# Grouped query pairs share value products, attention's scratch changes place, and norm squares are added on VectorE, in a two-layer hybrid trunk

## The chip, the core and the metric

The kernel runs on one core of a Trainium2 chip. The metric is the device time of one execution in microseconds (us), the median of several runs. The engines are TensorE (PE: matrix products; its weight loads are listed as PEld), VectorE (DVE), ScalarE (ACT), GpSimd (POOL) and SyncE (SP), whose queue starts all transfers. PSUM is the memory that TensorE writes, in banks; SBUF is the working memory.

## The reference

Two layers over 256 context tokens and 512 latent tokens of width 1024. In each layer a modulated RMS norm feeds one wide projection. Its columns go to four mixers (a bidirectional state-space layer "S5", a gated short convolution, neighbourhood attention, windowed grouped-query attention), to their gates and to merge gates. Each mixer's output is gated, projected and added into a sum that is gated by channel; one output projection and a gated residual end the layer. The parts that matter here, cut:

```python
def _rmsnorm(x, g):
    y = xf * lax.rsqrt(jnp.mean(xf * xf, axis=-1, keepdims=True) + EPS)
...
# grouped-query attention: 8 query heads, 2 key/value heads, blocks of 128 queries,
# keys: the block and its neighbours in a window of 128, the context, and a sink logit
pr = jax.nn.softmax(jnp.concatenate([s_lat, s_ctx, sink_l], axis=-1), axis=-1)
o = (jnp.einsum("bkgqs,bskd->bqkgd", pr[..., :span], v_i)
     + jnp.einsum("bkgqc,bckd->bqkgd", pr[..., span:span + n_ctx], v_ctx))
...
gated = y * jax.nn.silu(z[name + "_gate"])
contrib = jax.nn.sigmoid(z["merge_" + name]) * (gated @ p["w_br"][k])
```

The last layer computes its context tokens only as far as keys, values and states need them.

## The kernel before

Activations lie transposed: 128 channels on the partitions, tokens along the free dimension, the 1024 channels in 8 tiles. Large products run at a reduced-precision type in three terms: activations and weights are split into a high and a low part (`split`, line 228, a ScalarE cast and a VectorE subtraction), and `dense` (line 190) issues high x high, high x low and low x high. A unit of projection is 24 products over 512 latent tokens (bank `pl`) and, where the context is wanted, 24 over its 256 tokens (`pc`). Weights come through two buffers `wraw`.

A layer has two stages. `front` (line 685) runs attention. For each of 8 attention units (4 of neighbourhood attention, 4 grouped ones, each a pair of query heads) `weave` (line 777) interleaves query tiles of attention with projection units of the coming attention unit, convolution and gates. `back` (line 1350) runs the branch products (`merge`, line 1314), the S5 layer and the output projection, with the next layer's state-space factors (`s5_ahead`) between.

No engine order is written out: the program is traced with priorities, and a planner, which times instructions by a model of its own, fixes each engine's order when the program is built. Attention has a raised priority (`tile_prio`). Each engine then runs its own list in order, and waits on semaphores.

`attend_` (line 563) handles one head and 128 queries: scores into the bank pair `S`, bias and maximum on VectorE (line 576), exponentials on ScalarE (586), normalization on VectorE (588), transposes in blocks of 128 keys into `T` (597), a split into `ph` and `pl_` (two buffers each), and then the value products of line 606: per key block, 64 columns of high values with `ph` and with `pl_`, and 64 columns of low values with `ph`, added up in `o[:64, :128]` of the bank `M`, of which there is one. `store_y` (line 611) copies the sum to `y` on ScalarE (line 624). `M` also takes the sums of squares of the query/key norm (`qk_unit`, line 485) and of the token norm. Query stacks `qs0`, `qs1` have one buffer each and are filled by transfers from `qhi` and `qlo` (line 524).

`norm_stats` (line 351) makes the token norm's scale: ScalarE squares of each of the 8 tiles (line 359), then for each 128 tokens a product of the squares with a column of ones into `M` (line 364), a VectorE reduction over the 8 sums (375), a scalar step (377), the power -1/2 on GpSimd (379), transposes to spread it (382) and a copy (384). Another branch (`rows`) serves the latent tokens at the very start only. `norm_apply` (line 387) then multiplies, modulates and splits, tile by tile. Between the layers the latent tokens are normalized while the output projection still runs over the context for tiles 4 to 7.

SBUF pools are stacked. When the front's pool `at_` closes, the back's pools take its addresses: first `ac_` (accumulators `acc`), then `bm_` (the gated values `gh` and `gl`, loaded from memory). With `reuse_waits="tile"` a new tile waits for the last use of the old tiles that it overlaps. Within a pool, tiles lie in the order in which their names are first asked for.

Of the kernel before, what the change touches and what calls it, by code (L numbers as in the profile page):

```python
# [11 lines left out]
F32 = mybir.dt.float32  # L12
F32R = mybir.dt.float32r
AF = mybir.ActivationFunctionType
OP = mybir.AluOpType
# [3 lines left out]
D = 1024  # L19
SEQ = 512  # L20
CTX = 256
TOK = CTX + SEQ
NEG = -1e30
EPS = 1e-6
# [98 lines left out]
class Net:  # L123
# [227 lines left out]
    def norm_stats(self, pool, xs, q, rows=False):  # L351

        nc = self.nc
# [3 lines left out]
        for k in range(KD):  # L357
# [5 lines left out]
            for b in range(nb):  # L363
                nc.tensor.matmul(sums[:, b * 8 + k:b * 8 + k + 1], sq[:, b * 128:(b + 1) * 128], self.ones[:, 0:1],  # L364
                                 start=True, stop=True)
        t = pool.tile([128, 8], F32, name="ntiny", bufs=4)
        if rows:
# [5 lines left out]
            nc.vector.tensor_copy(t[:, :nb], sums[:, :nb])  # L373
        else:
# [185 lines left out]

    tile_prio = 1500

    def attend_(self, pool, qs, kh, kl, v, qtok, k0, vbs, bias, sink, dst):
# [25 lines left out]
        ph = pool.tile([128, 640], F32R, name="ph", bufs=2)  # L589
        pl = pool.tile([128, 640], F32R, name="pl_", bufs=2)  # L590
        vbs = (*vbs, 0, 1)
        nb = len(vbs)
        for b0 in range(0, nb, 4):
# [5 lines left out]
            self.split(ph[:, c], pl[:, c], T[:, :(b1 - b0) * 128])  # L599
        o = self.ps.tile([128, 512], F32, name="M")  # L600
        i = 0
        for b in range(nb):
            vb = vbs[b]
            c = slice(b * 128, (b + 1) * 128)
            for w, p in ((slice(0, 64), ph), (slice(0, 64), pl), (slice(64, 128), ph)):
                last = nc.tensor.matmul(o[:64, :128], v[:, vb, w], p[:, c], start=i == 0, stop=i == 3 * nb - 1)  # L606
                i += 1
        self.last_pv = last.ins
        dst(o[:64, :128])

    def store_y(self, y, h, j, na):
# [3 lines left out]
        def f(o):  # L615
            a = CTX - self.base
            if j < 0:
# [24 lines left out]
    def na_tiles(self, l, pool, m, parts, A):  # L642
        nc = self.nc
        A["y"] = y = self.tp(pool, "y", bufs=2)
        for h in range(2):
            args = (pool, A["qs"][h], A["kh"][h], A["kl"][h], A["v"][:, :, h])
            for j in range(4):
# [824 lines left out]
```

## Time and profile before

| | |
|---|---|
| median of 3 runs | 2159.69 us |
| the runs | 2159.69, 2160.14, 2150.65 us |
| profiled execution, its own time | 2153.59 us |
| its span in the profile | 2151.7 us |
| mean granted clock of TensorE | 0.982 |
| TensorE busy | 2086.2 us (97%) |
| VectorE busy | 1351.8 us (63%) |
| ScalarE busy | 898.2 us (42%) |
| GpSimd busy | 321.5 us (15%) |

Times inside the span count from its start. The front of layer 0 runs to about 650 us, its back to about 1290, the front of layer 1 to about 1770. A record of a product has the length of its way through the array, so records overlap; the time that a product holds TensorE is the distance to the next start. A product of the full-precision type has two records.

### The profile page before, as it was taken

What the parts mean: (1) busy time and instruction counts of PE and PEld (TensorE: products, weight loads), DVE (VectorE), ACT (ScalarE), POOL (GpSimd) and SP (SyncE); (2) the same over time, 40 slices, a digit from 0 to 9 for tenths busy, and PEclk for the clock granted to TensorE, in tenths of its full rate; (3) what the DMA queues carried; (4) which work ended last, traced back from release to release, by engine and by line L of the source; (5) the groups of instructions that cost most, each with busy time, mean ns of one, the idle gap of its engine ahead of it and who ended that gap; (6) DMA issues with size and microseconds to landing.
All of it is one profiled execution on the core that took longest, in us unless ns stands there. A gap on an engine that the chain in (4) does not pass through costs nothing.

```text
span 2151.7 us, 34689 instructions
## 1 busy us (share of the span) xinstructions
PE 2086.2 (97%) x12868; PEld 1784.2 (83%) x12868; DVE 1351.8 (63%) x2770; ACT 898.2 (42%) x1936; POOL 321.5 (15%) x326
## 2 busy tenths in 40 slices
PE   8899999999999999999899998999999999999999
PEld 3788888898898888888788887888888887878887
DVE  6476767579665778777547764455556655566543
ACT  4454444354643333333333335455445453323331
POOL 1721222232310000000000004222223300000000
PEclk9899999999999999999999989999999999999999
DMA  6353553532424556464254755444333328863542
GB/s 257 118 154 115 155 159 108 155 121 65 136 82 159 148 157 187 131 182 128 83 192 143 241 178 193 132 122 128 95 113 97 118 91 258 263 204 112 167 138 98
DMA packets 165774, 316.45 MB, mean 147 GB/s; under 512 B 59363, under 2 KB 83171, under 8 KB 164837
## 3 DMA queue, kind: packets, MB, share of 16 engines
q1 hardware_dynamic: 165604, 314.24, 47.6%
q8 instruction: 101, 1.65, 0.3%
q14 instruction: 69, 0.56, 0.1%
HBM read 214.09 MB, written 51.31 MB: 123 GB/s over the span
## 4 chain that ended last, share of the span: by engine, by line
PE 69%; DVE 5%; DMA 4%; ACT 2%; issue 1%; SPq 1%; POOL 0%; DVEq 0%; ACTq 0%; POOLq 0%
PE pl L209 36%; PE pc L209 10%; PE S L209 9%; PE M L606 3%; PE T L597 2%; DMA s<-s 2%; PE T L1076 2%; PE S L570 1%; PE T L1150 1%; PE S L572 1%; PE T L1067 1%; PE M L485 1%; PE T L1193 0%; PE T L1192 0%; PE M L364 0%
## 5 line engine op out<-in xcount | busy, mean ns | idle before, releaser
L209 PE MATMUL pl<-hh,whi 128*128 128x512 f32 x1312 | 522.9, 400 | 5.0 <-ACT hh L229 2.2
L209 PE MATMUL pl<-hh,wlo 128*128 128x512 f32 x1312 | 522.0, 398 | 5.5 <-DVE wlo L178 5.5
L209 PE MATMUL pl<-hl,whi 128*128 128x512 f32 x1312 | 522.8, 398 | 1.1 <-DVE hl L230 1.1
L177 ACT CAST whi<-wraw 128x512 fp32r<-128x512 f32 x440 | 271.8, 620 | 505.6 <-PE pl L209 196.6
L178 DVE TENSOR_TENSOR wlo<-wraw,whi 128x512 fp32r<-128x512 f32 x348 | 241.4, 696 | 185.6 <-ACT whi L177 180.3
L209 PEld LDWEIGHTS pl<-hh,wlo 128*128 128x128 f32 x1312 | 247.6, 189 | 58.4 <-DVE wlo L178 6.8
L209 PEld LDWEIGHTS pl<-hh,whi 128*128 128x128 f32 x1312 | 247.8, 189 | 54.6 <-ACT hh L229 3.6
L209 PEld LDWEIGHTS pl<-hl,whi 128*128 128x128 f32 x1312 | 247.9, 189 | 51.1 <-DVE hl L230 2.5
L209 PE MATMUL pc<-hh,whi 128*128 128x256 f32 x768 | 224.3, 292 | 8.5 <-ACT hh L229 4.5
L209 PE MATMUL pc<-hl,whi 128*128 128x256 f32 x768 | 221.2, 288 | 1.0 <-DVE hl L230 0.9
L209 PE MATMUL pc<-hh,wlo 128*128 128x256 f32 x768 | 220.8, 287 | 0.0
L178 POOL TENSOR_TENSOR wlo<-wraw,whi 128x512 fp32r<-128x512 f32 x92 | 127.6, 1390 | 305.2 <-ACT whi L177 259.8
L209 PEld LDWEIGHTS pc<-hh,whi 128*128 128x128 f32 x768 | 147.8, 192 | 17.5 <-ACT hh L229 5.9
L586 ACT ACTIVATE s<-s,stiny 128x512 f32<-128x512 f32 (+2 forms) x160 | 112.5, 703 | 108.9 <-DVE stiny L585 54.6
L209 PEld LDWEIGHTS pc<-hl,whi 128*128 128x128 f32 x768 | 147.6, 192 | 7.3 <-DVE hl L230 2.1
L606 PE MATMUL M<-ph,v 128*64 128x128 f32 x1216 | 147.2, 228 | 4.1 <-ACT y L624 1.8
L209 PEld LDWEIGHTS pc<-hh,wlo 128*128 128x128 f32 x768 | 147.5, 192 | 0.9 <-issue 0.4
L209 PE MATMUL S<-gh,whi 128*128 128x512 f32 (+1 forms) x384 | 138.8, 361 | 2.2 <-DMA gh<-gd 0.8
L209 PE MATMUL S<-gl,whi 128*128 128x512 f32 (+1 forms) x384 | 137.7, 359 | 1.4 <-DMA gl<-gd 1.4
L209 PE MATMUL S<-gh,wlo 128*128 128x512 f32 (+1 forms) x384 | 137.2, 357 | 0.0
L606 PEld LDWEIGHTS M<-ph,v 128*64 128x64 f32 x1216 | 127.2, 138 | 12.0 <-ACT y L624 3.3
L229 ACT CAST ph<-T 128x512 fp32r<-128x512 f32 (+2 forms) x192 | 92.7, 497 | 57.3 <-PE T L597 50.3
(778 smaller groups left out, 3733.6 us busy)
## 6 DMA issues: line engine op xcount, KB each, us to landing
wraw<-wu SPq DMA_DIRECT2D x220, 512.0 KB
wada<-wada SPq DMA_DIRECT2D x40, 512.0 KB
s<-s SPq DMA_DIRECT2D x80, 192.0 KB
bias<-bias SPq DMA_DIRECT2D x64, 128.0 KB
kh<-qhi SPq DMA_DIRECT2D x40, 192.0 KB
kl<-qlo SPq DMA_DIRECT2D x40, 192.0 KB
gh<-gd SPq DMA_DIRECT2D x16, 384.0 KB
gl<-gd SPq DMA_DIRECT2D x16, 384.0 KB
```

Source lines behind the costliest of these rows:

```text
L177: nc.scalar.copy(hi, raw[:, c])
L178: e.tensor_tensor(lo, raw[:, c], hi.bitcast(F32), op=OP.subtract)
L209: mm = nc.tensor.matmul(out[q], a[:, c], b[k][:, s], start=k + n == 0, stop=k == nk - 1 and n == 2)
L229: self.nc.scalar.copy(hi, src)
L485: nc.tensor.matmul(sums[:, 2 * b:2 * b + 2], sq[:, c:c + 128], self.blk1, start=True, stop=True)
L570: nc.tensor.matmul(S[:, 512 - n:512], qa, k[:, CTX + k0 * 64:CTX + k0 * 64 + n], start=i == 0, stop=i == 1)
L572: nc.tensor.matmul(S[:, 512:768], qa, k[:, :CTX], start=i == 0, stop=i == 1)
L586: nc.scalar.activation(s[:, a:e], s[:, a:e], AF.Exp, bias=tn[:, 1:2], accum_out=tn[:, 2:3])
L597: nc.tensor.transpose(T[:, (b - b0) * 128:(b - b0 + 1) * 128], s[:, a + b * 128:a + (b + 1) * 128], self.ident)
L606: last = nc.tensor.matmul(o[:64, :128], v[:, vb, w], p[:, c], start=i == 0, stop=i == 3 * nb - 1)
L1067: nc.tensor.transpose(o[:, g * 128:(g + 1) * 128], win[d][:, g].rearrange("p s i -> p (s i)"), self.ident)
L1076: nc.tensor.matmul(o[:16, g * 128:(g + 1) * 128], X[:, 0, d, g], WO[:, d, g, d:d + 8].rearrange("p k i -> p (k i)"), start=True, stop=True)
```

## The change

Four edits. In the grouped attention units the two heads of a pair, which share keys and values, are now visited in turn for each query tile; their probabilities lie in two halves of one pair of tiles, and one set of products of 128 value columns (high and low) by 256 (both heads' queries) serves both. The rows for low values times low probabilities come along. The upper 64 rows of the result are added to the lower on VectorE as the result is stored. Neighbourhood attention keeps its products and alternates the halves. In `norm_stats` the 8 tiles of squares are added on VectorE and one product per 128 tokens sums over the channels. In `front`, the scratch of convolution and of query normalization is asked for first, so it lies lowest in the pool. The accumulators' pool is opened after `bm_` rather than before.

```diff
@@ norm_stats
-            for b in range(nb):
-                nc.tensor.matmul(sums[:, b * 8 + k:b * 8 + k + 1], sq[:, b * 128:(b + 1) * 128], self.ones[:, 0:1],
-                                 start=True, stop=True)
+            if k == 0:
+                tot = sq
+            elif k == 1:
+                t1 = pool.tile([128, 512], F32, name="nsum", bufs=1)[:, :n]
+                nc.vector.tensor_tensor(t1, tot, sq, op=OP.add)
+                tot = t1
+            else:
+                nc.vector.tensor_tensor(tot, tot, sq, op=OP.add)
...
         else:
-            nc.vector.tensor_reduce(t[:, :nb], sums[:, :8 * nb].rearrange("p (b k) -> p b k", k=8),
-                                    axis=mybir.AxisListType.X, op=OP.add)
-        nc.vector.tensor_scalar(t[:, :nb], t[:, :nb], 1.0 / D, EPS, op0=OP.mult, op1=OP.add)
+            for b in range(nb):
+                nc.tensor.matmul(sums[:, b:b + 1], tot[:, b * 128:(b + 1) * 128], self.ones[:, 0:1], start=True, stop=True)
+            nc.vector.tensor_scalar(t[:, :nb], sums[:, :nb], 1.0 / D, EPS, op0=OP.mult, op1=OP.add)
@@ attend_, and the new values_
-        ph = pool.tile([128, 640], F32R, name="ph", bufs=2)
-        pl = pool.tile([128, 640], F32R, name="pl_", bufs=2)
+        ph, pl = (t[:, half] for t in self.pt)
...
+    def values_(self, v, vbs, half, dsts):
+        nc = self.nc
+        ph, pl = self.pt
+        vbs = (*vbs, 0, 1)
         o = self.ps.tile([128, 512], F32, name="M")
-            for w, p in ((slice(0, 64), ph), (slice(0, 64), pl), (slice(64, 128), ph)):
-                last = nc.tensor.matmul(o[:64, :128], v[:, vb, w], p[:, c], start=i == 0, stop=i == 3 * nb - 1)
-                i += 1
+        for b, vb in enumerate(vbs):
             c = slice(b * 128, (b + 1) * 128)
+            if half is None:
+                for i, p in enumerate((ph, pl)):
+                    last = nc.tensor.matmul(o[:, :256], v[:, vb], p[:, :, c], start=b + i == 0, stop=b == len(vbs) - 1 and i == 1)
+                continue
+            for i, (w, p) in enumerate(((slice(0, 64), ph), (slice(0, 64), pl), (slice(64, 128), ph))):
+                last = nc.tensor.matmul(o[:64, :128], v[:, vb, w], p[:, half, c], start=b + i == 0, stop=b == len(vbs) - 1 and i == 2)
         self.last_pv = last.ins
-        dst(o[:64, :128])
+        for h, dst in enumerate(dsts):
+            dst(o[:, h * 128:(h + 1) * 128], half is None)
@@ store_y
             nc.scalar.copy(d, o)
+            if two:
+                nc.vector.tensor_tensor(d, d, o2, op=OP.add)
@@ na_setup
+        self.pt = [pool.tile([128, 2, 640], F32R, name=n) for n in ("ph", "pl_")]
@@ gqa_tiles
+        for j in (0, 1, 2, 3) + ((-2, -1) if "c" in parts else ()):
...
+            for h in range(2):
...
+                self.attend(pool, A["qs"][h], A["kh"][kv], A["kl"][kv], h, qtok, 2 * k0, vbs, mask, sink)
+                if h == 1:
+                    self.values(v, vbs, None, [self.store_y(y, i, j, False) for i in range(2)])
                 yield
@@ front
+        self.t3(pool, "cvv", bufs=1), self.tp(pool, "cvy", bufs=1)
+        for _ in range(3):
+            self.t3(pool, "qt", bufs=3)
+        for n in ("qhi", "qlo"):
+            self.t3(pool, n, bufs=1, dt=F32R)
         self.attention_constants(pool)
@@ back
             pm = stack.enter_context(tc.tile_pool(name=f"bm_{l}", bufs=1, reuse_waits="tile"))
+            self.pacc = stack.enter_context(tc.tile_pool(name=f"ac_{l}", bufs=1, reuse_waits="tile"))
@@ body
-                net.pacc = stack.enter_context(tc.tile_pool(name=f"ac_{l}", bufs=1, reuse_waits="tile"))
```

`na_tiles` calls `attend` and then `values` with its own half and one destination.

## Rows read from the trace of the kernel before

**Rows 1.** The page: TensorE's share of the span; its granted clock in 40 slices.
```profile
PE 2086.2 (97%) x12868; PEld 1784.2 (83%) x12868; DVE 1351.8 (63%) x2770; ACT 898.2 (42%) x1936; POOL 321.5 (15%) x326
...
PEclk9899999999999999999999989999999999999999
```

**Rows 2.** List of waits of TensorE: total us, times, longest.
```profile
PE S L570 <- DMA qs<-qlo: 5.0, 4, 1.9
...
PE M L606 <- ACT y L624: 1.8, 5, 0.5
```

**Rows 3.** Windows of the grouped stretches: length, busy per engine, clock, transfer share, GB/s.
```profile
405.00:525.00 120.00, 116.25 (x844) 104.09 (x843) 99.90 (x313) 55.60 (x140) 33.68 (x41) 0.99 0.32 103
...
1580.00:1772.00 192.00, 189.95 (x1322) 165.39 (x1321) 113.87 (x268) 96.55 (x220) 49.91 (x63) 1.00 0.31 96
```

**Rows 4.** The page's costliest groups: the value products with `ph`.
```profile
L606 PE MATMUL M<-ph,v 128*64 128x128 f32 x1216 | 147.2, 228 | 4.1 <-ACT y L624 1.8
```

**Rows 5.** Timeline of TensorE, 562 to 568 us: start, length, instruction.
```profile
562.25 0.22 PE L606 MATMUL M<-ph,v 128*64 128x128 f32 x1
...
563.15 0.34 PE L570 MATMUL S<-kh,qs 128*128 128x256 f32 x1
...
564.74 0.28 PE L209 MATMUL pc<-hh,whi 128*128 128x256 f32 x1
...
567.62 0.39 PE L209 MATMUL pl<-hh,whi 128*128 128x512 f32 x1
```

**Rows 6.** Durations of small ScalarE and VectorE instructions, by line and timeline.
```profile
L624 ACT COPY y<-M x160: 240/258/265, 124.4 to 1770.9; 64x128 f32<-64x128 f32 x160
...
L1081 DVE TENSOR_TENSOR sln<-sln,T x16: 198/202/210, 705.9 to 1281.8; 16x64 f32<-16x64 f32 x16
...
1260.12 0.28 DVE L1032 TENSOR_TENSOR sX<-smt,skl 128x128 f32<-128x128 f32 x1
...
L1176 DVE TENSOR_TENSOR s<-s,s x16: 415/418/421, 736.2 to 1960.0; 128x256 f32<-128x256 f32 x16
...
L178 DVE TENSOR_TENSOR wlo<-wraw,whi 128x512 fp32r<-128x512 f32 x348 | 241.4, 696 | 185.6 <-ACT whi L177 180.3 <-PE pl L209 2.1 <-DMA bias<-bias 1.0
```

**Rows 7.** Timeline of TensorE between the layers.
```profile
1258.94 1.05 PE L1076 MATMUL T<-sWO,sX 128*16 128x128 f32 x8
...
1262.82 2.73 PE L364 MATMUL M<-ones,nsq 128*128 128x1 f32 x24
...
1274.07 1.89 PE L1076 MATMUL T<-sWO,sX 128*16 128x128 f32 x8
...
1283.96 0.60 PE L382 MATMUL T<-kc,ntiny 128*128 128x128 f32 x4
...
1291.48 0.48 PE L209 MATMUL pl<-hh,whi 128*128 128x512 f32 x1
```

**Rows 8.** Windows of line 364 alone: length, PE, PEld, clock, transfers.
```profile
43.00:53.00 10.00, 3.84 (x32) 3.96 (x32) 1.00 0.00 1
1262.00:1277.00 15.00, 9.18 (x56) 9.60 (x56) 0.67 0.47 163
```

**Rows 9.** Windows between the layers, columns as in rows 3.
```profile
1260.00:1270.00 10.00, 10.00 (x65) 9.46 (x66) 9.45 (x20) 4.13 (x7) 0.00 (x0) 0.86 0.43 131
1270.00:1280.00 10.00, 10.00 (x46) 8.66 (x47) 1.25 (x4) 3.10 (x7) 1.01 (x1) 0.50 0.35 141
```

**Rows 10.** Timelines of VectorE and GpSimd between the layers.
```profile
1263.02 0.75 DVE L1398 SCALAR_TENSOR_TENSOR gl<-pl,mod,gl 128x512 f32<-128x512 f32 x1 [0.34 <-PE pl L209]
...
1277.13 1.01 POOL L379 TENSOR_TENSOR ntiny<-ntiny,kc 128x4 f32<-128x4 f32 x1 [251.70 <-DMA wd<-sWT]
...
1285.71 3.53 DVE L391 TENSOR_TENSOR nh<-gh,nrs 128x512 f32<-128x512 f32 x2
```

**Rows 11.** Window in the prologue, columns as in rows 3.
```profile
50.00:60.00 10.00, 4.80 (x23) 2.70 (x20) 9.13 (x26) 4.04 (x7) 0.70 (x1) 0.77 0.00 1
```

**Rows 12.** Timeline of TensorE at layer 1's first branch product.
```profile
1785.49 0.50 PE L209 MATMUL S<-gl,whi 128*128 128x512 f32 x1 [1.09 <-DMA gl<-gd]
```

More of the change, by code (lines that the diff above doesn't have):

```diff
@@ L373, in norm_stats @@
             nc.vector.tensor_copy(t[:, :nb], sums[:, :nb])
+            nc.vector.tensor_scalar(t[:, :nb], t[:, :nb], 1.0 / D, EPS, op0=OP.mult, op1=OP.add)
         else:
-            nc.vector.tensor_reduce(t[:, :nb], sums[:, :8 * nb].rearrange("p (b k) -> p b k", k=8),
-                                    axis=mybir.AxisListType.X, op=OP.add)
-        nc.vector.tensor_scalar(t[:, :nb], t[:, :nb], 1.0 / D, EPS, op0=OP.mult, op1=OP.add)
+            for b in range(nb):
+                nc.tensor.matmul(sums[:, b:b + 1], tot[:, b * 128:(b + 1) * 128], self.ones[:, 0:1], start=True, stop=True)
+            nc.vector.tensor_scalar(t[:, :nb], sums[:, :nb], 1.0 / D, EPS, op0=OP.mult, op1=OP.add)
         r = pool.tile([128, 8], F32, name="ntiny", bufs=4)
@@ L559, in attend, with values, attend_ @@
             self.attend_(*args)
+    def values(self, *args):
+        with self.tc.high_priority(offset=self.tile_prio):
+            self.values_(*args)
     tile_prio = 1500
-    def attend_(self, pool, qs, kh, kl, v, qtok, k0, vbs, bias, sink, dst):
+    def attend_(self, pool, qs, kh, kl, half, qtok, k0, vbs, bias, sink):
         nc = self.nc
@@ L613, in store_y, with f @@
         part = y[h * 64:(h + 1) * 64]
-        def f(o):
+        def f(o, two):
             a = CTX - self.base
+            o, o2 = o[:64], o[64:]
             if j < 0:
@@ L644, in na_tiles @@
         A["y"] = y = self.tp(pool, "y", bufs=2)
+        half = 0
         for h in range(2):
-            args = (pool, A["qs"][h], A["kh"][h], A["kl"][h], A["v"][:, :, h])
-            for j in range(4):
-                b = self.biases[self.nbias % 2]
-                self.nbias += 1
-                k0, vbs = NA_KEYS[j]
-                nc.sync.dma_start(b[:, 128:384], self.ap["bias"][l, 2 * m + h, j])
-                self.attend(*args, CTX + j * 128, k0, vbs, b[:, 128:], None, self.store_y(y, h, j, True))
+            v = A["v"][:, :, h]
+            for j in (0, 1, 2, 3) + ((-2, -1) if "c" in parts else ()):
+                args = (pool, A["qs"][h], A["kh"][h], A["kl"][h], half)
+                if j >= 0:
+                    b = self.biases[self.nbias % 2]
+                    self.nbias += 1
+                    k0, vbs = NA_KEYS[j]
+                    nc.sync.dma_start(b[:, 128:384], self.ap["bias"][l, 2 * m + h, j])
+                    self.attend(*args, CTX + j * 128, k0, vbs, b[:, 128:], None)
+                else:
+                    vbs = ()
+                    self.attend(*args, (j + 2) * 128, 0, vbs, self.zeros, None)
+                self.values(v, vbs, half, (self.store_y(y, h, j, True),))
+                half = 1 - half
                 yield
-            if "c" in parts:
-                for j in (-2, -1):
-                    self.attend(*args, (j + 2) * 128, 0, (), self.zeros, None, self.store_y(y, h, j, True))
-                    yield
         self.dump(f"yna{l}{m}", y)
```

24 lines of the change are left out of this document (8 added, 16 removed).

## The prediction

> **What bounds the kernel.** I read the page first. TensorE is busy 97% of the span, at a granted clock of 9 tenths or more in all but one of the 40 slices [rows 1]. What counts is therefore the time each instruction holds TensorE, from its start to the start of the next one. An instruction taken from another engine counts only where TensorE waits for it. Next came the list of waits: its entries for TensorE are a few microseconds each. It waited 5.0 us in all for the q stacks of attention and 1.8 us for the evacuation of the bank that value products write [rows 2]. Last came windows over the two stretches with grouped-query attention. TensorE is busy 116.3 of 120 us and 190.0 of 192 us there; VectorE is busy 99.9 of 120 us in the first, which is the densest, and 113.9 of 192 us in the second [rows 3]. So projections fill the gaps of attention, and TensorE work taken away there should come off the span.
>
> **Value products of grouped queries.** The page has 1216 products with `ph` [rows 4]; those with `pl_` are half as many (two of three operands are `ph`), so 1824 in all. By the code a grouped pair of heads has 22 key blocks over its six query tiles in layer 0 and 18 over its four in layer 1. With four pairs of heads that is 88 + 72 = 160 blocks. Each costs 6 instructions before (three per head) and 2 after: 960 go, 320 come. Fifteen products of 64 columns by 128 follow one another from 562.25 to 563.15 us, 0.060 us each. The 24 products of 128 columns by 256 right after run from 564.74 to 567.62 us, 0.120 us each [rows 5]. A new product has the latter's shape, so 960 x 0.060 - 320 x 0.120 = 57.6 - 38.4 = 19.2 us leave TensorE. The new shape's bounds hardly differ: both rows are from this kernel.
>
> The Trainium skill ("TensorE: Matmul & The Clock Gate", Back-to-back issue gap) says that in a stream of weight-load and product pairs a product is spaced by about 81 ns at 128 columns and 131 ns at 512. By that, with some 98 ns in between as my estimate for 256, the trade would be 77.8 - 31.4 = 46 us and the result 2103. The rows show 60 ns at 128, so I give that outcome no chance of its own.
>
> What comes with it: a pair's evacuation was two ScalarE copies of 0.258 us out of two separate uses of the bank. It becomes copy, VectorE add, copy, VectorE add on one use. VectorE gets 80 adds of 64x128. The trace has none of that shape from PSUM; below it lies 16x64 from PSUM at 0.202 us, above it 128x128 at 0.28 us [rows 6]. I take 0.28: 22 us on VectorE, 13 of them in layer 0, where it is 83% busy at the worst. These hide behind projections on TensorE; where they delay a softmax, TensorE stalls. Also, both heads' q stacks are now read until the last tile of a unit, so the first head's next stack is loaded later; before, only the second head's was. There are three such changes of unit per layer. I charge 2 us for the adds and the bank (bounds 0 and 8) and 1 us for the stacks (0 and 4, from 0.7 us for each of six).
>
> **Norm squares.** Three sums of squares take the changed branch: the context's at the start, and the latent and the context one between the layers. Each had 8 products of one column per 128 tokens, 64 in all, each appearing as two records. 8 products remain. Between the layers this matters most. From 1262.82, when the last latent output product is out, to 1291.48, the first projection of layer 1, TensorE never rests [rows 7]. In it 56 one-column records are 9.2 us of its time [rows 8], and 12 of the 32 context records another 1.3. For these come 8 records, 0.9 us at 24 in 2.6 us [rows 7]. In the same stretch the granted clock is 0.86 and then 0.50, that is 1.2 GHz in the second window [rows 9], after 48 one-column records. Eight 16-wide products took 1.89 us there against 1.05 in the same shape at full clock [rows 7]. Over the two such groups, two groups of transposes and 12 products of 256 the loss is about 3.6 us, an estimate from those rows. If it goes with its cause, 28.7 - 9.2 - 1.3 + 0.9 - 3.6 = 15.5 us of work remain, ending at 1278.3: 13 us earlier.
>
> That needs the normalized tokens by then. The last latent output is added to x at 1263.02 + 0.75 [rows 10]. Square, last add and four products take some 2.3 us, the scalar step and the power 1.2 (the power 1.01 [rows 10]). From the transposes at 1283.96 to the projection at 1291.48 it was 7.5 us [rows 7]. Sum: 1263.8 + 11 = 1274.8, before TensorE runs out. The new adds are seven of 128x512, 0.696 us by the nearest row, and seven of 128x256, 0.418 [rows 6]: 4.9 + 2.9 us of VectorE. It is 94% busy from 1260 to 1270 with state-space factors and then 12% to 1280 [rows 9]. If all seven latent adds were ordered behind the factors, from 1270.2, the tokens would be ready 1270.2 + 4.9 + 0.9 + 1.2 + 7.5 = 1284.7. TensorE would then wait 6.4 us and 7 remain of the 13. I take 12 us for the stage, bounds 5 and 15 (the upper one with the other 20 context records, 2.1 us).
>
> The Trainium skill ("SBUF — State Buffer", Who interferes with whom) speaks against such adds: a VectorE instruction with two SBUF inputs contends with a GpSimd instruction that reads SBUF. The trace agrees: two 128x512 products took 3.53 us while GpSimd worked, where 0.69 each is usual [rows 6, 10]. By it the seven latent adds would take 12 us, not 4.9. But GpSimd had been idle for 251.7 us when the power came [rows 10], so the latent adds have the ports alone. Only the context's may meet it.
>
> At the start 3.8 us of records go [rows 8], but there TensorE is busy 4.8 of 10 us while VectorE, which makes the modulation, is busy 9.1 [rows 11]. Seven adds more on VectorE cost up to 2.9 us, the earlier sums give up to 3 back: 0, bounds -3 and +3.
>
> **Addresses.** The gated values' tiles come to lie on scratch of convolution and query normalization, the accumulators behind them. In layer 1 the first branch product waited 1.09 us for a gated value [rows 12]; this and two neighbours sum to 2.7 us. In layer 0 no such wait exists. But three of layer 1's eight first loads then fall on the masks and the probabilities, which live to the end of attention. I take 1.5 us of gain, bounds 0 and 2.7.
>
> **Sum.** -19.2 + 2 + 1 - 12 + 0 - 1.5 = -29.7 us. The profiled execution took 2153.6 us, 1.9 more than its span, and would come to 2123.9. Its time is 6.1 us under the median of 2159.7, which two of three runs share; against that median I forecast 2130.
>
> **Rivals.** 0.5% of the median, 10.8 us, is about what a measurement of this kernel can tell from no change.
>
> *The norm's gain is half hidden.* VectorE takes the adds after the factors, and the stage gives 5 us: -22.7, so 2137. For it: a fixed order per engine, and VectorE's 94%. Against it: VectorE had been idle for 0.34 us when the last output came [rows 10].
>
> *The shared evacuation becomes the wait.* This is the case on the other side. The next pair's products and the query norm's sums need the same single bank, now behind two ScalarE and two VectorE turns, and a pair's probabilities are overwritten only when both heads' products are done. There are 40 pairs. A wait of 0.5 us each returns 20 us: 2150. At 0.74 us the change breaks even, and from (29.7 + 10.8) / 40 = 1.0 us each the kernel is slower by over 0.5%. With the two copies and two adds wholly exposed, 2 x 0.258 + 2 x 0.28 = 1.1 us each, it takes 2159.7 - 29.7 + 44 = 2174. For it: VectorE at 83%. Against it: 1.8 us of waiting for that bank in the whole run [rows 2] and about 10 us between pairs.
>
> *The order is made anew.* A planner fixes each engine's order, and the change moves most of it; weight loads may come late. TensorE's waits for stacks are 5.0 us in all now [rows 2]; for late weights I know no nearer measure than the same again. Ten more gives 2140, ten less 2120.
>
> **Chances.** Forecast 0.60 (own range 2120 to 2151 by its bounds: all on the gain side -39.9, all on the other -9.2), norm half hidden 0.14, evacuation wait 0.14 (slower 0.06, about the same 0.06, faster 0.02), new order 0.12 (faster 0.08, same 0.04). Faster by over 0.5%: 0.60 + 0.14 + 0.02 + 0.08 = 0.84; same 0.10; slower 0.06. The range reaches from the gain-side bounds with a favourable new order, 2120 - 10 = 2110, to the other bounds, 2159.7 - 9.2 = 2150.5, which takes in the evacuation case at 0.5 us a pair; beyond lie the slower cases and what I have not thought of, under 2 in 10.
>
> **What would show it.** Grouped products in runs of two per block 0.120 us apart; TensorE busy in the grouped stretches as before but these 19 us shorter in sum; no entry of half a microsecond per pair on the value bank in the list of waits; between the layers a granted clock near 1.0 and layer 1's first projection 12 us sooner after the last latent output product. Wrong would make it: waits of TensorE on the added copies, or a longer VectorE chain before layer 1.

## The result, and the profile after

The changed kernel takes 2175.7 us (median of 6 runs, 2171.4 to 2181.4) against 2156.3 for the kernel before beside it: a ratio of 1.0089, 95% interval 1.0072 to 1.0106. It is slower by 19 us; forecast was 30 us faster. The profiled execution took 2175.1 us with a span of 2173.2, against 2153.6 and 2151.7.

The page of the changed kernel, its first row and the granted clock:

```profile
PE 2069.3 (95%) x12116; PEld 1753.5 (81%) x12116; DVE 1378.5 (63%) x2868; ACT 896.6 (41%) x1936; POOL 322.4 (15%) x326
...
PEclk9899999999999999999999989999999998999999
```

Against [rows 1] TensorE is busy 16.9 us less, so some of the work did go. But its idle time, span less busy time, grew from 65.5 to 103.9 us: 38.4 more. The two make the 21.5 us by which the span is longer. Of the 38.4 us of idle time 9.7 lie before layer 0's first branch product, 8.8 between the layers and 17.6 in the grouped stretch of layer 1. Windows of the changed kernel, columns as in [rows 3]; the first two are the stretches of [rows 3], the next three lie between the layers [rows 9], the last three are the end of layer 1's attention and the first branch products:

```profile
405.00:525.00 120.00, 116.66 (x712) 103.16 (x711) 100.62 (x320) 53.15 (x131) 31.55 (x39) 0.97 0.32 103
1580.00:1772.00 192.00, 182.21 (x995) 154.42 (x994) 118.75 (x281) 92.66 (x206) 48.04 (x61) 1.00 0.30 95
...
1260.00:1270.00 10.00, 10.00 (x71) 9.01 (x72) 9.04 (x22) 6.57 (x16) 0.41 (x1) 1.00 0.65 228
1270.00:1280.00 10.00, 7.15 (x61) 6.94 (x60) 10.00 (x17) 5.27 (x12) 5.52 (x3) 0.98 0.69 218
1280.00:1290.00 10.00, 5.87 (x30) 3.97 (x30) 5.42 (x10) 3.35 (x6) 2.92 (x2) 0.67 0.63 213
...
1771.00:1783.00 12.00, 9.90 (x58) 8.35 (x57) 6.51 (x18) 4.79 (x12) 0.18 (x1) 0.93 0.26 88
1783.00:1800.00 17.00, 8.99 (x39) 6.07 (x38) 3.24 (x7) 5.00 (x12) 1.48 (x3) 0.70 0.59 194
1800.00:1820.00 20.00, 16.48 (x64) 12.54 (x63) 10.76 (x15) 5.33 (x10) 0.25 (x3) 0.70 0.71 212
```

In the second stretch TensorE now stands for 9.8 of 192 us (2.0 before). Between the layers the removed products have become waits. From 1771 to 1800 it is busy 18.9 of 29 us, and the granted clock of the two windows from 1783 to 1820 is 0.70, a mixture of the levels 2.4 and 1.2 GHz. In the kernel before, the same end of the stage:

```profile
1770.00:1782.00 12.00, 12.00 (x62) 9.89 (x61) 3.78 (x5) 6.15 (x12) 1.52 (x3) 1.00 0.63 224
1782.00:1800.00 18.00, 14.96 (x64) 11.33 (x63) 8.41 (x10) 5.24 (x10) 0.18 (x3) 0.91 0.90 282
...
1771.26 1.30 POOL L421 TENSOR_TENSOR gt<-gt,y 128x512 f32<-128x512 f32 x1 [25.26 <-ACT y L624]
...
1782.63 0.39 PE L209 MATMUL S<-gh,whi 128*128 128x512 f32 x1
```

There TensorE is busy without a gap from the last unit's gate (1771.26) to the first branch product (1782.63). The largest waits of TensorE in the list of waits:

```profile
PE S L209 <- DMA gh<-gd: 12.7, 2, 7.3
...
PE pl L209 <- ACT hh L229: 5.0, 2, 4.2
```

Both are at the ends of stages: for gated values ahead of each layer's first branch product, and for normalized tokens ahead of layer 1. The timeline at layer 1's first branch product (start, length, instruction, in brackets the idle time before and its releaser):

```profile
1789.01 1.26 POOL L428 TENSOR_TENSOR gt<-gt,y 128x512 f32<-128x512 f32 x1 [12.21 <-DVE y L645]
...
1790.30 0.62 ACT L229 CAST ghi<-gt 128x512 fp32r<-128x512 f32 x1 [1.70 <-POOL gt L428]
...
1790.94 0.33 SPq L436 DMA_DIRECT2D gd<-ghi  x1
...
1792.04 0.45 SPq L1354 DMA_DIRECT2D gh<-gd  x1
...
1795.03 0.80 PE L209 MATMUL S<-gh,whi 128*128 128x512 f32 x1 [7.33 <-DMA gh<-gd]
```

The last unit's result y, its gate, the stores (`gd`) and the loads (`gh`) follow one another, and no projection is left to cover them; in the kernel before projections filled this stretch. The loads are issued behind the last gate's store, so other addresses could not make them earlier.

A pair in the densest part of layer 0, timeline of three engines (dense projections and most other instructions left out):

```profile
541.40 0.28 PE L621 MATMUL M<-pl__441,v 128*128 128x256 f32 x1
...
541.52 0.27 PE L621 MATMUL M<-ph,v 128*128 128x256 f32 x1
...
541.63 0.28 PE L621 MATMUL M<-pl__441,v 128*128 128x256 f32 x1
...
542.11 1.54 DVE L945 TENSOR_TENSOR mt<-wadaj 128x256 f32<-128x256 f32 x1
542.16 0.26 ACT L643 COPY y<-M 64x128 f32<-64x128 f32 x1
...
543.57 0.41 DVE L230 TENSOR_TENSOR pl__441<-T,ph 128x256 fp32r<-128x256 f32 x1
544.01 0.29 DVE L645 TENSOR_TENSOR y<-y,M 64x128 f32<-64x128 f32 x1
...
544.34 0.26 ACT L643 COPY y<-M 64x128 f32<-64x128 f32 x1 [1.65 <-DVE y L645]
...
545.56 1.27 DVE L940 TENSOR_TENSOR wadaj<-mt 128x192 f32<-128x192 f32 x1
...
546.75 0.35 DVE L942 TENSOR_TENSOR wadaj<-mt 128x192 f32<-128x192 f32 x1
547.12 0.29 DVE L645 TENSOR_TENSOR y<-y,M 64x128 f32<-64x128 f32 x1
```

The products are 0.12 us apart, as forecast. The four evacuations last 0.26 or 0.29 us each, but the bank is free only at 547.41, 5.78 us after the last product began. The adds queue on VectorE behind state-space preparation (L940 to L945) and a split (L230), and ScalarE's second copy waits 1.65 us for the first add. Over layer 0's 24 pairs this time is 4.4 us on average; before, it was 0.94 us from a tile's last product to the end of its single copy, so 1.9 for two tiles.

### The profile page after: what moved, and what is told of

It reads as the page before. It is cut to its first block, busy times and chain, and to the rows that moved or that the text cites. A ratio compares the mean times of both kernels' runs of the same rounds, so it can differ in the third digit from the quotient of the medians.

```text
span 2173.2 us, 33327 instructions
## 1 busy us (share of the span) xinstructions
PE 2069.3 (95%) x12116; PEld 1753.5 (81%) x12116; DVE 1378.5 (63%) x2868; ACT 896.6 (41%) x1936; POOL 322.4 (15%) x326
## 4 chain that ended last, share of the span: by engine, by line
PE 73%; DVE 10%; DMA 7%; issue 4%; ACT 3%; SPq 2%; POOL 1%; DVEq 0%; ACTq 0%; POOLq 0%
PE pl L209 38%; PE pc L209 12%; PE S L209 8%; DMA s<-s 3%; PE T L606 2%; PE M L624 2%; PE S L583 1%; PE T L1108 1%; PE S L581 1%; PE M L492 1%; PE M L621 1%; DVE wadaj L325 1%; DMA qs<-qlo 1%; PE T L1182 1%; DVE wlo L178 1%
## 5 line engine op out<-in xcount | busy, mean ns | idle before, releaser
L597 ACT ACTIVATE s<-s,stiny 128x512 f32<-128x512 f32 (+3 forms) x160 | 112.7, 704 | 115.4 <-DVE stiny L593 57.9
L229 ACT CAST ph<-T 128x512 fp32r<-128x512 f32 (+1 forms) x192 | 93.1, 496 | 77.9 <-PE T L606 64.1
L209 PEld LDWEIGHTS S<-gh,whi 128*128 128x128 f32 x384 | 74.0, 193 | 35.8 <-DMA gh<-gd 15.4
L606 PE MATMUL T<-kc,s 128*128 128x128 f32 x608 | 99.4, 276 | 3.6 <-DVE pl__13531 L230 1.4
```

Source lines behind the costliest of these rows:

```text
L209: mm = nc.tensor.matmul(out[q], a[:, c], b[k][:, s], start=k + n == 0, stop=k == nk - 1 and n == 2)
L229: self.nc.scalar.copy(hi, src)
L597: nc.scalar.activation(s[:, a:e], s[:, a:e], AF.Exp, bias=tn[:, 1:2], accum_out=tn[:, 2:3])
L606: nc.tensor.transpose(T[:, (b - b0) * 128:(b - b0 + 1) * 128], s[:, a + b * 128:a + (b + 1) * 128], self.ident)
```

## Experiments

The table is worked out from the timelines of each kernel's profiled execution. Bank: time from the start of the last value product to the end of its last evacuation, mean over layer 0's grouped tiles, per pair of tiles. Stages in us: A from the start to layer 0's first branch product; B from there to the last latent output product; C from there to layer 1's first projection; D from layer 1's first grouped score product to its first branch product; E from there to the end of TensorE's last product. The neighbourhood attention of layer 1, between C and D, is not listed. Ratios are medians of 4 to 10 runs against the kernel before on the same chip; the stages come from one execution each.

```
kernel          ratio   bank    A      B      C     D      E
before          1       1.9   690.9  571.7  28.9  200.2  365.3
addr_only       1.0009  1.9   691.9  570.5  28.9  202.0  369.9
norm_only       0.9981  1.9   694.4  568.3  27.6  200.6  370.0
norm_s          0.9954  1.9   695.0  568.8  17.5  199.6  367.3
changed         1.0089  4.4   693.0  569.8  29.1  213.9  374.5
pair_only       1.0074  4.5   688.2  569.3  29.0  214.4  371.3
no_addr         1.009   4.4   688.1  568.3  27.3  215.7  376.8
no_adds         0.9944  1.5   693.8  560.4  27.2  207.8  371.8
sum_pool        0.9963  2.2   685.3  561.3  28.8  207.6  373.7
sum_pool_s      0.9952  2.1   694.6  561.1  17.8  208.0  370.7
two_copies      0.9998  3.4   690.1  569.6  29.0  204.5  370.7
free_add        0.9998  4.3   690.1  569.2  30.1  207.6  364.6
copy_v          1.0012  4.0   693.3  562.6  30.0  209.5  374.9
interleave      0.9968  2.0   695.5  560.6  27.5  204.0  368.3
inter_s         0.995   2.0   689.9  560.7  17.3  203.9  368.3
few_products    0.9861  2.4   677.6  561.0  27.5  191.4  370.3
hold            1.0137  2.4   719.6  562.3  26.8  217.8  369.0
one_half        1.019   2.0   729.7  567.1  27.6  212.6  373.5
per_head        1.0264  4.4   726.9  568.2  30.3  215.8  371.9
per_head_pool   1.0018  3.0   702.7  560.4  27.8  209.4  365.8
```

### The parts alone

pair_only and no_addr differ from the changed kernel by these lines taken back:

```diff
# pair_only: norm_stats as before, and as in no_addr
# no_addr:
-        self.t3(pool, "cvv", bufs=1), self.tp(pool, "cvy", bufs=1)
...
-            self.pacc = stack.enter_context(tc.tile_pool(name=f"ac_{l}", ...))
+                net.pacc = stack.enter_context(tc.tile_pool(name=f"ac_{l}", ...))
# norm_only: the kernel before with norm_stats as changed
# addr_only: the kernel before with the lines that no_addr takes back
```

pair_only: 

> The kernel before with the grouped pairs alone (shared value products, paired probability tiles); norm and addresses as before. Theory, the time went into the attention units: a unit now ends later and its q stacks come free later, so the dense work beside it runs out and TensorE idles ahead of layer 1's first branch product; the 19 us of removed products do not show, and the run is 5 to 20 us slower than before, with the unit starts of layer 1's grouped stretch about 12 us apart from those of before by the last unit. Rival, the pairs are worth their 19 us and something else costs: 2135 to 2145. Rival, the shared bank makes TensorE wait 0.5 us or more for each of 40 pairs: waits of the value products on the copies of 20 us in sum.

norm_only: 

> The kernel before with the norm squares added on VectorE, the rest as before. Theory, the stretch between the layers is set by the chain through VectorE and by the order of the transposes: about the time of before (within 4 us), the removed one-column products turned into waits of TensorE of 5 us or more there. Rival, the stage is worth its forecast 12 us when nothing else is changed: 2140 to 2146.

addr_only: 

> The kernel before with the tiles' addresses alone changed (order of allocation in the front, accumulators after the merge tiles). Theory: within 3 us of before, since the loads of gated values stand behind the last gate's stores in SyncE's order. Rival, the addresses are what costs: 10 to 20 us slower, with the 7 us wait for gated values ahead of layer 1's first branch product.

no_addr: 

> The changed kernel with the old addresses: pairs and norm squares together. Theory (attention units): as the changed kernel within 5 us, 2170 to 2180. Rival, the addresses cost: 2130 to 2145. Rival, the planner's order decides and each small difference moves the time by 10 us either way: it lies away from the sum of the two parts by that much.

Measured: pairs alone 1.0074 (1.0045 to 1.0104), 16 us slower; norm squares alone 0.9981 (0.9966 to 0.9996), 4 us faster; addresses alone 1.0009 (0.9997 to 1.0022); pairs and norm squares 1.009 (1.0068 to 1.0113). The loss is the pairs'. It repeats where it lies: stage D is 213.9 to 215.7 in the three kernels with pairs and adds, 199.6 to 202.0 in the four with the old products and order. Layer 0's stage A holds 10.6 us of the removed products and is shorter by 2.8 at most. Stage E is longer than before by 6.0 to 11.5 in these three, but by 4.6 and 4.7 with the addresses or the norm squares alone as well, so not all of that is the pairs'.

### Pairs against the heads' own products

```diff
# interleave
-                if h == 1:
-                    self.values(v, vbs, None, [self.store_y(y, i, j, False) for i in range(2)])
+                self.values(v, vbs, h, (self.store_y(y, h, j, False),))
# per_head: heads one after the other, alternate halves, and
+                    last = nc.tensor.matmul(o[:, :128], v[:, vb], p[:, half, c], ...)
# one_half: heads one after the other, own products, without
-            half = 1 - half
# no_adds
-            if two:
-                nc.vector.tensor_tensor(d, d, o2, op=OP.add)
```

interleave: 

> The changed kernel with the two heads still taken in turn for each query tile, but with value products for each head as before (three for a key block, own evacuation, no add): 960 products again. Both heads' q stacks are held to the unit's end, and the probabilities of a tile come free with its own products. Theory Q: slow, 2170 or above (it lacks the saving too). Theory P: near the kernel before, 2150 to 2163. Theory A: near the kernel before as well.

per_head: 

> The changed kernel, but grouped queries go one head after the other as before, and each head has its own value products: the 128 columns of v (high and low half) against 128 probabilities of one head, two products for a key block where the kernel before has three; one copy and one add for each head's tile. TensorE work removed is of the same order as with pairs, and so many adds as there. Theory P (with pairs a tile's probabilities come free only after both heads' products, so that the chain of attention is one tile deep in place of two): the gain stays, 2130 to 2152. Theory Q (the q stacks are held to the unit's end): the same, 2130 to 2152. Theory A (the adds on VectorE and the longer evacuation cost): slow as the changed kernel, 2165 to 2180.

one_half: 

> The changed kernel, with heads one after the other and value products as before (three for a key block, no pairs, no adds) in grouped attention, but all of these tiles put their probabilities into one half of the probability tiles, so that a tile's are overwritten only after its products. Theory P: slower than before by 10 us or more, 2165 to 2190, with waits of the splits for value products and small idle times of TensorE in layer 1's grouped stretch. Theories Q and A: within 6 us of the kernel before, 2150 to 2163.

no_adds: 

> The changed kernel without the 80 VectorE adds of the second half of the values' bank (the low half of v is left out of the grouped queries' result). Theory A: 2150 or below. Theories P and Q: within 6 us of the changed kernel, 2168 to 2180.

Measured: interleave 0.9968 (0.995 to 0.9985), per_head 1.0264 (1.0225 to 1.0303), one_half 1.019 (1.0152 to 1.0227), no_adds 0.9944 (0.9923 to 0.9965). Theory Q falls as the main cause: with the stacks held to the unit's end the kernel is no slower, though stage D is 2 to 4 us longer than with the old order and a stage B 11 us shorter than before hides some of it. Theory A holds in its direction: without the adds 31 us go, 0.0145 of the time, of which 9 lie in stage B; per_head, where each of 80 tiles has its own copy and add, is the slowest of all, 31 us beyond the theory's range. Theory P has support too: tiles that share one half of the probabilities cost 41 us against the kernel before, which takes the heads in the same sequence.

per_head does not show that no hold is needed to lose, because its products are not what its expectation says. Products of 128 columns of v by 128 queries follow one another 0.11 us apart, not 0.060; the 0.060 us were of products with 64 columns. From the page of per_head_pool, which has the same products, and its timeline, then from the page of interleave:

```profile
PE 2086.2 (97%) x12436; PEld 1781.6 (83%) x12436; DVE 1359.6 (63%) x2788; ACT 921.0 (43%) x2016; POOL 365.1 (17%) x406
...
528.37 0.28 PE L621 MATMUL M<-pl__441,v 128*128 128x128 f32 x1
528.49 0.27 PE L621 MATMUL M<-ph,v 128*128 128x128 f32 x1
528.60 0.28 PE L621 MATMUL M<-pl__441,v 128*128 128x128 f32 x1
```
```profile
PE 2078.0 (97%) x12756; PEld 1773.8 (83%) x12756; DVE 1352.9 (63%) x2788; ACT 899.0 (42%) x1936; POOL 323.0 (15%) x326
```

640 such products take some 70 us in place of 58 for 960: TensorE is busy 8.2 us longer in per_head_pool, not 19 us less.

### What it is about the adds

```diff
# copy_v: the first copy on VectorE too
-            nc.scalar.copy(d, o)
+            if two:
+                nc.vector.tensor_copy(d, o)
...
# two_copies
-                nc.vector.tensor_tensor(d, d, o2, op=OP.add)
+                nc.scalar.copy(d, o2)
# free_add
-                nc.vector.tensor_tensor(d, d, o2, op=OP.add)
+                nc.vector.tensor_tensor(self.spare, self.zeros[:64, :128], o2, op=OP.add)
# sum_pool
-                nc.vector.tensor_tensor(d, d, o2, op=OP.add)
+                nc.scalar.copy(two[h * 64:(h + 1) * 64], o2)
+                if h:
...
+                    nc.gpsimd.tensor_tensor(y[:, c], y[:, c], two, op=OP.add)
```

copy_v: 

> The changed kernel with the first halves of the pairs' bank copied by VectorE in place of ScalarE: copy and add follow on one engine, 160 VectorE instructions of some 0.28 us in place of 80, and no VectorE instruction of the evacuation waits for ScalarE. Theory H1 (the adds cost because VectorE, in order, stands at an add until ScalarE's copy is done, and the softmax behind it stands too): 2145 to 2163. Theory H2 (the adds cost by their own time on VectorE): 2190 or above. Theory H3 (the bank is held by some 1.1 us of evacuation for each pair and the next products wait for it): as the changed kernel, 2168 to 2182.

two_copies: 

> The changed kernel with each add replaced by a second ScalarE copy into the same place (the sum of the halves is left out): nothing on VectorE, no engine waits for another within the evacuation, the bank is held for four copies, some 1.04 us. H3: as the changed kernel, 2168 to 2182. H1 and H2: near the run without adds, 2140 to 2155.

free_add: 

> The changed kernel with each add made independent of ScalarE's copy: it adds the second half of the bank to zeros into a tile that nobody reads (the sum of the halves is left out). 80 VectorE adds of the same size, the bank read by both engines, no wait of one for the other. H1: 2140 to 2158. H2: as the changed kernel, 2168 to 2182. H3: between, as the bank is held for about half of the time, 2155 to 2168.

sum_pool: 

> The changed kernel with the whole result kept: ScalarE copies both halves out of the bank (four copies for each pair), and GpSimd adds them from its own copy, one add of 128x128 for each pair; VectorE has no part. H1 and H2: near the run without adds, 2140 to 2155, faster than the kernel before. H3: 2165 to 2182.

Measured: copy_v 1.0012 (0.9996 to 1.0027), two_copies 0.9998 (0.9982 to 1.0014), free_add 0.9998 (0.998 to 1.0017), sum_pool 0.9963 (0.9946 to 0.9981). H2 falls: twice the VectorE instructions are 17 us faster than the changed kernel (7 of them in stage B). H3 alone falls too: in free_add the bank is taken as long as in the changed kernel, 4.3 us, and 20 us are gone (the time lies in H3's range, but the shorter hold that the range was worked out from is not there). H1 gave the times of free_add and copy_v to within two microseconds; two_copies is 5 us above its range. But free_add did not take away the wait that H1 speaks of. Each of its 80 adds starts after ScalarE's copy out of the same bank has ended, and each next copy after the add, as in the changed kernel. One pair of free_add, then the list of one line, the adds of the changed kernel and those of free_add, with VectorE's idle time ahead of them:

```profile
541.90 0.26 ACT L643 COPY y<-M 64x128 f32<-64x128 f32 x1
...
542.49 0.29 DVE L645 TENSOR_TENSOR spare<-kb,M 64x128 f32<-64x128 f32 x1
...
542.81 0.26 ACT L643 COPY y<-M 64x128 f32<-64x128 f32 x1 [0.39 <-DVE spare L645]
```

```profile
L645 DVE TENSOR_TENSOR y<-y,M x80: 289/291/294, 429.2 to 1788.6; 64x128 f32<-64x128 f32 x80
...
  ACT y L643: 17.4, 17
```
```profile
L645 DVE TENSOR_TENSOR spare<-kb,M x80: 280/290/292, 430.1 to 1782.2; 64x128 f32<-64x128 f32 x80
...
  ACT y L643: 16.6, 13
```

VectorE stands for ScalarE as long in both, so H1 stays untested there. What the runs show is that VectorE's adds onto y behind ScalarE's copies cost 17 to 31 us against each of five other evacuations; 7 to 9 of these belong to stage B in three of them (below), which leaves 9 to 22 us. How much is wait or order they do not separate. That the bank's hold sets it is not borne out: with pairs and no such add stage D is 204.5 to 208.0 us in five kernels, whether the bank is taken for 1.5 us (no_adds) or 4.3 (free_add).

### TensorE's time, the hold, and the bank of the norm

```diff
# few_products, on interleave
+                last = nc.tensor.matmul(o[:64, :128], v[:, vb, :64], ph[:, half, c], ...)
+                continue
# norm_s, on norm_only
-        rb = self.ps.tile([128, 512], F32, name="T", bufs=2)
+        rb = self.ps.tile([128, 1024], F32, name="S")[:, :512] if pool.name != "pro" else ...
# hold, on interleave
-                self.values(v, vbs, h, (self.store_y(y, h, j, False),))
+                for i in (1, 0) if h else ():
+                    self.values(v, vbs, i, (self.store_y(y, i, j, False),))
# per_head_pool, on interleave
+                    last = nc.tensor.matmul(o[:, :128], v[:, vb], p[:, half, c], ...)
...
+                nc.scalar.copy(two, o2)
+                nc.gpsimd.tensor_tensor(d, d, two, op=OP.add)
# sum_pool_s and inter_s: sum_pool and interleave with the lines of norm_s and no_addr
```

few_products: 

> The interleaved run with the value products of grouped queries cut to one of three for a key block (high half of v by high half of the probabilities; the two low terms are left out of the result): 640 products of 0.060 us, 38 us of TensorE time less than there, everything else the same. Theory K (the grouped stretches end when attention's chain over VectorE and ScalarE ends, some 20 us before the first branch product in layer 0 and 7.5 in layer 1; TensorE is busy with projections that run ahead): at most 8 us below the interleaved run, 2138 to 2152. Theory PE (TensorE's time sets these stretches, as the prediction had it): 2105 to 2118.

hold: 

> The interleaved run with one thing changed: both heads' probabilities of a query tile are made first, then come the products of the second head and, in the bank after those, the products of the first, so that the first head's probabilities are held as long as in a pair. 960 products, no adds. Theory P (a pair's hold of the probabilities eats the saving): 10 us or more above the interleaved run, 2158 to 2175. Rival (the hold costs nothing; the saving is lost in the bank's longer evacuation): within 5 us of it, 2143 to 2154.

per_head_pool: 

> The interleaved run with two products of 128 columns for a key block of one head in place of three (all 128 columns of v as weights: 640 products of 0.060 us, 19 us less TensorE time, as much as pairs remove), the low half copied out by a second ScalarE copy and added on GpSimd; no hold by the other head. Theory P: 8 to 19 us below the interleaved run, 2130 to 2141. Rival (the second copy, that is the bank's evacuation, eats it): within 5 us of the interleaved run, 2143 to 2154.

norm_s: 

> The run with the norm squares alone, and the transposes of the norm's factors between the layers in bank S, which is free there, in place of the bank T that state-space transposes take in turn. Theory T (the latent tokens' transposes stand behind state-space transposes that took the bank first and wait for VectorE): layer 1's first projection comes 6 to 12 us sooner after the last latent output product than with the norm squares alone, and the run takes 2138 to 2146. Rival (the adds' own time on VectorE, or the chain from sums to projection, sets it): as with the norm squares alone, 2148 to 2156.

sum_pool_s: 

> Pairs with the halves added on GpSimd, norm squares with the transposes in bank S, and the old addresses. If the parts add up: 4 us for the old addresses and 6 to 12 for the bank come off sum_pool, 2134 to 2146. If each new order throws its own few microseconds: 2140 to 2158.

inter_s: 

> Heads in turn with products of their own (960 again, no adds), norm squares with the transposes in bank S, and the old addresses. If the parts add up: 2134 to 2145, level with sum_pool_s within 6 us though it has 19 us more of TensorE work. If TensorE's time counted, it would be 15 us or more above sum_pool_s.

Measured: few_products 0.9861 (0.9833 to 0.9889), hold 1.0137 (1.0102 to 1.0171), per_head_pool 1.0018 (0.9996 to 1.004), norm_s 0.9954 (0.9936 to 0.9972), sum_pool_s 0.9952 (0.993 to 0.9974), inter_s 0.995 (0.9931 to 0.9969).

few_products misses both its theories: 38 us of TensorE time bring 23. By stage, A gives 17.9 of the 21.1 removed there, D 12.6 of 17.3. So a tile's products do count. hold shows what a pair's hold can cost: 24 us in A and 14 in D for the same instructions as interleave, beyond theory P's range (with it goes that the first head's products wait for the bank of the second's). per_head_pool settles nothing on the hold: its products take 8 us more of TensorE than interleave's, not 19 less (above), and it is 11 us slower, which neither theory had. Its second copy and GpSimd's adds come on top; the run does not separate them.

Read together: these stretches follow attention's own sequence of softmax, split, products and evacuation. Work taken out of one tile's products shortens it; a hold of the probabilities lengthens it. A pair does the one by 0.48 us and the other as well. The start of stage D's last score product shows it, in us from the start of the stage: 167.9 before, 175.3 in interleave, 189.5 to 192.5 in the five kernels with pairs and no add onto y, 195.5 in the changed kernel, 196.4 in hold. From there to the first branch product projections cover 32.3 us before and only 18.4 in the changed kernel, so 27.6 us of delay become 13.7 in the stage. Of these 13.7 some 4 come with heads in turn (interleave), some 4 with the pairs (sum_pool, 207.6, though interleave has 8.6 us more of products there) and some 6 with the adds. That the hold is what delays the pairs is argued from the run hold; no run has pairs without it.

norm_s, TensorE between the layers:

```profile
1269.09 0.94 PE L383 MATMUL M<-ones,nsum 128*128 128x1 f32 x8
...
1274.74 0.60 PE L389 MATMUL S<-kc,ntiny 128*128 128x128 f32 x4
...
1281.28 1.11 PE L209 MATMUL pl<-hh,whi 128*128 128x512 f32 x2 [2.77 <-ACT hh L229]
```

And the changed kernel, TensorE, then GpSimd and VectorE:

```profile
1268.06 0.95 PE L383 MATMUL M<-ones,nsum 128*128 128x1 f32 x8
...
1275.25 0.60 PE L1099 MATMUL T<-kc,swin 128*128 128x128 f32 x4
...
1279.88 1.11 PE L1099 MATMUL T<-kc,swin 128*128 128x128 f32 x4 [2.85 <-DVE swin L1082]
...
1284.45 1.03 PE L1108 MATMUL T<-sWO,sX 128*16 128x128 f32 x8 [1.01 <-DVE sWO L1082]
...
1286.24 1.40 PE L389 MATMUL T<-kc,ntiny 128*128 128x128 f32 x6 [0.76 <-ACT sln L1111]
...
1291.81 1.22 PE L209 MATMUL pl<-hh,whi 128*128 128x512 f32 x2 [4.17 <-ACT hh L229]
```
```profile
1269.59 2.61 POOL L386 TENSOR_TENSOR ntiny<-ntiny,kc 128x4 f32<-128x4 f32 x1 [241.85 <-DMA sTT<-sln]
1274.62 3.33 POOL L178 TENSOR_TENSOR wlo<-wraw,whi 128x512 fp32r<-128x512 f32 x2 [2.42 <-ACT whi L177]
...
1270.92 0.41 DVE L371 TENSOR_TENSOR nsum<-nsum,nsq 128x256 f32<-128x256 f32 x1
...
1274.31 0.42 DVE L371 TENSOR_TENSOR nsum<-nsum,nsq 128x256 f32<-128x256 f32 x1
...
1275.31 1.51 DVE L371 TENSOR_TENSOR nsum<-nsum,nsq 128x256 f32<-128x256 f32 x1
```

The latent factors are there at 1272.2 in the changed kernel, but their transposes (L389) come at 1286.2, behind state-space transposes that were given bank T first and wait for VectorE. In bank S they start at 1274.7, and the first projection comes 17.5 us after the last latent output product in place of 27.6: theory T has the stage right. The run gains 6 us of these 10 over norm_only and at 2148.0 us misses theory T's range by 2, at the edge of the rival's. sum_pool_s and inter_s are level, though TensorE has 19 us more of value products in inter_s, but neither adds up: they beat the kernel before by 0.5%, the changed one by some 1.4%, and are no better than norm_s alone.

## Why the prediction was wrong, step by step

**The premise was too strong: 19.2 us of value products forecast to come off the span, nothing seen.** "TensorE work taken away there should come off the span" was read from a busy share of 97%. The value products' size was right, 0.120 us each. TensorE's busy time fell by 16.9 us in all, where these and the one-column records (13.4 by the prediction's terms) were to take 32.6; the mean granted clock of 0.975 against 0.982 is worth some 15 us of that difference, by my estimate. But a busy TensorE was running projections ahead of need; when attention took longer, these ran out and the engine stood at the end of each front, where the gate, its stores and the loads of gated values follow one another. In layer 1 stage D became 13.7 us longer, and E 9.2, of which the pairs' share is open (above). The premise holds better for work that leaves a tile's products and delays nothing: few_products got 23 us for 38. Where the adds onto y are left out or replaced (no_adds, two_copies, free_add, sum_pool), the kernels with pairs lie within 3 us of the kernel before, stage B aside: the 19 us do not show there either.

**The adds and the bank: 2 us charged (bounds 0 and 8), 17 to 31 measured, 9 to 22 of them outside stage B.** This is the term that made the change a loss: none of the five kernels with another evacuation is slower than before by more than 0.12%. I priced the instructions, 0.28 us each (measured 0.29), and let them hide; their queueing on a VectorE 84% busy made an evacuation of 4.4 us of one of 1.1. That the longer evacuation is what costs is not shown, since free_add keeps it and is as fast as the kernel before. What the pairs delay without any add, 189.5 to 192.5 us to the last score against 175.3, had no term at all: the prediction names the hold of the probabilities in a rival and prices only the bank. My second rival, the shared evacuation, met the time with its 2174, but by luck: it wanted 44 us of TensorE waits on the value bank, and the list of waits has 1.4 us of them, none by a pair's products. The loss shows as units that start later (the fourth grouped unit of layer 1 starts 161.3 us into stage D, 136.3 before), then as idle time at the end.

**The q stacks: 1 us (0 to 4).** Stage D of interleave is 2 to 4 us longer than in the four kernels with the old order; the whole run shows no loss, with a stage B 11 us shorter.

**The norm squares: 12 us forecast (5 to 15), 4 measured.** (Ahead of the window at 0.50 lie 40 one-column records, not 48.) I looked at VectorE's order and not at the bank: the step that failed is the sum 1263.8 + 11, which lets the transposes follow the power at once. In the changed kernel 14.0 us lie between the two (1272.2 to 1286.2), a term that the prediction put at nothing; the sums and the power come 5 us later than it had them, and from the transposes to the projection it is 5.6 us, not 7.5. Of the rivals the half-hidden gain came nearest, by another mechanism. With bank S stage C is 11.4 us shorter than before, as forecast, and half is then given back: the first attention score of layer 1 comes 78.6 us after the last latent output product, 84.8 before. The Trainium skill ("SBUF — State Buffer", Who interferes with whom) says that a VectorE instruction with two SBUF inputs contends with a GpSimd instruction that reads SBUF. The trace agrees for one context add, 1.51 us beside a GpSimd split; another, at 1270.92 beside the power, kept its 0.41, and there the power took longer (below).

**The addresses: 1.5 us of gain forecast, none measured** (1.0009, 0.9997 to 1.0022). The wait of 1.09 us in [rows 12] was not the first branch product's, which came at 1782.63 without one. The loads stand behind the last gate's stores in SyncE's order.

**The spacing of products.** The rows' 60 ns at 128, for which the prediction gave the outcome of 2103 us no chance, are of products with 64 weight columns. With 128 weight columns the runs show 0.11 us (above). The prices of the shapes that the change trades, 0.060 and 0.120 us, were right.

**The new order** was worth what its rival said, about ten microseconds: stage B, which the pairs do not touch, is 560 to 563 us in nine kernels and 567 to 572 in the eleven others, with a wait of TensorE of 3.6 to 4.2 us for state-space results in the long ones and of some 1.2 in the short ones. Which edit tips it is not settled; so differences of 8 us between single runs of the table are read by stage. Open too is why an add onto y costs 6 us more in stage D than one into a spare tile.

## What to carry to other kernels

A high busy share does not say that an engine's work is on the path: look how long before the end of the stage its last necessary instruction is, and what runs ahead as filler. An evacuation lasts as long as its queueing on the engines that do it: a copy and an add in turn, on ScalarE and on a VectorE that was 84% busy, took four times their instruction times. Before the number of products is traded, measure the spacing of the very shape, weight columns included. Before a transpose is moved earlier, see which bank it takes and whose turn that is.

## What was not expected of the hardware

The power of four columns on GpSimd took 2.61 us beside a VectorE busy 9.0 and 10.0 of 10 us in the two windows it lies in, against 1.01 before [rows 10], where VectorE was nearly idle. In norm_only, norm_s, sum_pool and interleave it took 2.61 or 2.62 as well. Products of 128 weight columns by 128 took 0.11 us each where those of 64 weight columns took 0.060, so that two of the one take longer than three of the other.
